# Value projections computed with tokens on the partitions, 512 weight columns per matmul

## The chip, the core and the metric

The kernel runs on one core of one Trainium2 chip. The metric is the device time of one execution in microseconds, the median of several runs. A profiled execution is one such run with the hardware profiler on; its span, from the first to the last recorded instruction, is a little shorter than the time measured for it.

## What is computed

Two layers of a decoder trunk over 256 tokens of 1024 channels. Each layer has a mixer (three branches A, B and C that share one input projection and are merged by gates) and a mixture-of-experts stage. The part that matters here:

```python
D_MODEL = 1024; SEQ = 256; DEPTH = 2          # BATCH = 1
DA_HEADS = 4;   DA_HEAD_DIM = 64;  DA_WIDTH = 512
SB_HEADS = 8;   SB_HEAD_DIM = 64;  SB_WIDTH = 512
CONV_CH = 512;  CONV_WIDTH = 31
IN_SIZES = (512, 512, 512, 2 * 512, 512, 512, 512, 3 * 1024)

def mixer(h, cos, sin, lambda_init, w_in, ...):
    proj = h @ w_in
    qa, ka, va, ub, qc, kc, vc, gates = jnp.split(proj, IN_SPLITS, axis=-1)
    qa = apply_rope(rms_norm(qa.reshape(B, S, 8, 64), qn_g), cos, sin)
    ka = apply_rope(rms_norm(ka.reshape(B, S, 8, 64), kn_g), cos, sin)
    va = va.reshape(B, S, DA_HEADS, 2 * DA_HEAD_DIM)
    ...
    y_a = diff_attention(qa, ka, va, lam, lambda_init, subln_g) @ w_proj_a
    y_b = conformer_conv(ub, w_dw, b_dw, conv_ln_g, conv_ln_b) @ w_proj_b + b_proj_b
    y_c = stick_breaking(qc, kc, vc) @ w_proj_c          # each (B, S, 8, 64)
    g = jax.nn.sigmoid(gates.reshape(B, S, 3, D_MODEL))
    merged = g[:, :, 0] * y_a + g[:, :, 1] * y_b + g[:, :, 2] * y_c
    return merged @ w_out

def conformer_conv(u, ...):
    a, g = jnp.split(u, 2, axis=-1)
    h = a * jax.nn.sigmoid(g)                  # then a causal depthwise convolution, 31 taps
    ...
    return jax.nn.silu(layer_norm(h, ln_g, ln_b))

for l in range(DEPTH):
    ...
    x = x + g_m * mixer(rms_norm(x, norm_mix_g[l]) * (1 + sc_m) + sh_m, ...)
    x = x + g_f * moe_ffn(rms_norm(x, norm_ffn_g[l]) * (1 + sc_f) + sh_f, ...)
```

`va` and `vc`, two of the eight slices of the input projection, are the values of the two attentions. An attention multiplies its weights, a matrix of keys by queries, with the values, and for that the values lie with the tokens on the partitions.

## The kernel before

**Layout.** Activations lie with channels on the partitions and the 256 tokens along the free dimension: `X[j]` is channel block j (128 channels, 8 blocks) of the normalised input. A block is kept either plain in f32, or as two parts in the fp32r format, `hH` (the rounded value) and `hL` (the rest); `plain(...)` and the table `NAT` say how many blocks are plain: none for the input projection of layer 0, three for that of layer 1. A product of split operands takes three fp32r matmuls (`mmj`: H with H, H with L, L with H), a plain one takes one f32 matmul, which runs as two passes and shows as two records. Weights that need it are split just ahead of use by `split`, into buffers named `WH` (an ACT copy) and `WL` (a DVE subtraction), each 128x512 elements; `NSPLIT` = 5 of them are in rotation, and `ahead` splits as far ahead as the buffers allow. `pieces` lists which pieces of a weight are split, in the order of use.

**Projections.** `proj_chunk` computes one chunk: 128 output channels by 256 tokens, with a 128x128 block of the weight as the stationary operand and `X[j]` as the moving one. Four PSUM banks with the name `psA` take these results. A projection such as `qa` has four chunks.

**Value projections.** `tokmajor(n)` computes the four chunks in the same way, channels on the partitions, copies each pair of them to `vT` (ACT), and then appends `flip_v` to the side work: four transposes on PE (L1056) into a bank of `psS`, `psT` or `psG`, and a copy on ACT into the final tile, with tokens on the partitions.

**Order of the work.** One function, `mixer_body`, writes out the order for each layer. `main()` emits the large matmuls and hands over after each chunk with two numbers, an estimate in microseconds of what the piece costs on PE and on DVE (`CH` for input chunks, `GH` for gate chunks). After each such hand-over a loop at the end of `mixer_body` does three things. It advances each generator in the list `sides` by a step (rotary embedding, attention heads, `sums` of squares, `flip_v`, `conv_norm`). It adds to a balance called `credit`: `credit += rate * pc - dc`. As long as the balance is positive, `fill_one` puts one piece of filler work on DVE and takes its cost off: alternately a row of the modulation product (`mod_fill`, `mod_dot`, L530) and a tap of the depthwise convolution (`conv_fill`, L762 and L765; 124 for each layer). Modulation rows that are due are put in even without credit, and then the balance goes negative. So the numbers handed over decide where fillers stand, and nothing measures the time while this is done.

When `conv_fill` is called once more behind the last tap, it appends `conv_norm` (L789 ff.) to the side work. That is the layer norm and the swish of branch B: the mean by four matmuls with `part`, a subtraction (L795), two squares on ACT (L798), sums over channels (`tok_sum`), eleven small DVE operations in `rsqrt` (L455 to L464), a diagonal (L486), a product with `ones` that spreads it over the partitions, four scalings (L813), four sigmoids on ACT and four products (L820). Its result is `T["ob"]`, the input of branch B.

The sequence of the large pieces is in `FRONT` (layer 0: qa, ka, va, ub, kc, qc, vc; layer 1: qa, va, ka, ub, qc, kc, vc) and `PLAN` (layer 0: acACbB, layer 1: abABcC; a small letter is the gate of a branch, a capital the branch's own projection). Then comes the output projection, `out`, and behind it the norm, the routing and the experts. `branch(br)` waits, while nothing else is emitted, as long as the branch's input does not exist (`yield STALL`); it then splits that input into `oH` and `oL` (L1239), multiplies, and merges the result with the gates (L1255, L1259, L1261).

Each engine executes its instructions in the order in which they were written. The weight transfers are issued by SyncE in an order of their own (`Stream`), five buffers deep.

Of the kernel before, what the change touches and what calls it, by code (L numbers as in the profile page):

```python
# [11 lines left out]
F32 = mybir.dt.float32  # L12
# [156 lines left out]
def trunk(ctx, tc, A, out, dbg=None):  # L169
# [426 lines left out]
    def mixer_body(l, pool, before=None):  # L596
# [6 lines left out]
        def take(k):  # L603
            while not free[k]:
                yield POLL
            return free[k].pop(0)
# [15 lines left out]
        def plain(kind, n):  # L622
            return NAT[l]["g" if n in GATES else "i" if kind == "in" else "o" if kind == "out" else n]

        def pieces(o):
            n = plain(*o[0:2])
            return [o + (hf,) for hf in range(2) if n < (4 if o[0] == "proj" else 4 * hf + 4)]
# [40 lines left out]

        def first_split(o):
            n = plain(*o[0:2])  # L670
            return min(4, n if o[0] == "proj" else max(n - 4 * o[3], 0))
# [7 lines left out]
        def split(o):  # L679
            if l == 0 and o[1] in FRONT[0][0:2]:  # L680
                release(o)
            j = first_split(o)
            H = pool.tile([P, 4, P], F32R, name="WH", bufs=NSPLIT[l])
            Lo = pool.tile([P, 4, P], F32R, name="WL", bufs=NSPLIT[l])
            src = weights(o)[:, j:]
# [365 lines left out]
        def flip_v(n, c, vT):  # L1051
            tag = yield from take("ps")
            bt = bank(tag)
            for t in range(NT):
                for k in range(2):
                    pe.transpose(out=bt[:, t * S + k * P:t * S + (k + 1) * P], in_=vT[:, k, t * P:(t + 1) * P],  # L1056
                                 identity=ident)
            yield .9, 0
            se.activation(T["t" + n][:, :, c * S:(c + 1) * S], c2(bt), AF.Copy)
            give("ps", tag)  # L1060
            if c == 1:
                T[n] = T["t" + n]

        def tokmajor(n):
            T["t" + n] = pool.tile([P, 2, 512], F32, name=n)
            for c in range(2):
                b = bank("A")
                for k in range(2):
                    proj_chunk(n, 2 * c + k, b)
                    if k == 0:  # L1070
                        yield CH
                vT = pool.tile([P, 2, S], F32, name="vT", tag="sg", bufs=4)
                se.activation(vT, c2(b), AF.Copy)
                yield CH
                sides.append(flip_v(n, c, vT))
# [17 lines left out]
        CH, GH = ((2.77 + .11 * NAT[l][k], 1.2 - .14 * NAT[l][k]) for k in "ig")  # L1093
        STALL = (.6, 0)
# [835 lines left out]
```

## Time and profile before

| | |
|---|---|
| median of 3 runs | 1621.5 us (1621.37 to 1621.63) |
| profiled execution, its own time | 1622.29 us |
| its span | 1620.7 us |
| PE busy | 1555.2 us (96%), 9710 instructions |
| DVE busy | 751.5 us (46%) |
| ACT busy | 469.1 us (29%) |
| DMA queue q1 | 542.31 MB, 82.5% of 16 engines' span |
| chain of work that ended last | PE 53%, DMA 40%, DVE 4% |

The shares are averages over two layers, each with a mixer and an experts' stage. Seen in 40 slices of the span, PE and DVE are both busy in the first fifth (the mixer of layer 0) and again around the middle (the mixer of layer 1), while the DMA rate falls there to 53 and 97 GB/s; in the rest, the experts, the transfers run at about 420 GB/s and DVE is busy for a fifth of the time. The matmuls of one line (L198, the helper that records every matmul) are told apart by their tiles.

### The profile page before, as it was taken

The numbers are of one execution on the slowest core, as the hardware profiler recorded it, in microseconds if no ns is written. First come the engines' busy times: TensorE is split into PE (matmuls) and PEld (weight loads), VectorE is DVE, ScalarE is ACT, GpSimd is POOL, SyncE is SP. The second block draws the span as 40 slices with busy tenths as digits, with TensorE's granted clock in tenths as the row PEclk, the third lists the DMA queues.
The fourth block names the chain that finished last, engine by engine and source line by source line (L and its number), as shares of the span: only waits on it lengthen the run. The fifth ranks groups of instructions, "written<-read, shape, count | busy, mean of one in ns | idle before, by whom it ended". The sixth has DMA issues, their size and how long they took to land.

```text
span 1620.7 us, 25003 instructions
## 1 busy us (share of the span) xinstructions
PE 1555.2 (96%) x9710; PEld 1050.0 (65%) x9710; DVE 751.5 (46%) x1866; ACT 469.1 (29%) x911; POOL 2.9 (0%) x26
## 2 busy tenths in 40 slices
PE   6999999999999999899989999999999999999997
PEld 5999869974554545454478888798745454554543
DVE  8799989652221222122249998554422222221122
ACT  3546833431111111111144355243211111111111
POOL 0000000000000000000000000000000000000000
PEclk9999979999999999999989999899999999999999
DMA  9985418959999999999958753256599999999997
GB/s 378 366 325 220 156 53 338 386 225 381 408 419 419 420 418 419 421 420 419 414 234 344 276 211 115 97 216 270 201 378 420 419 421 419 418 419 422 420 418 301
DMA packets 76154, 543.95 MB, mean 336 GB/s; under 512 B 8576, under 2 KB 9216, under 8 KB 12544
## 3 DMA queue, kind: packets, MB, share of 16 engines
q1 hardware_dynamic: 76032, 542.31, 82.5%
q8 instruction: 78, 1.28, 0.3%
q14 instruction: 44, 0.36, 0.1%
HBM read 541.23 MB, written 1.05 MB: 335 GB/s over the span
## 4 chain that ended last, share of the span: by engine, by line
PE 53%; DMA 40%; DVE 4%; ACT 1%; issue 1%; SPq 0%; DVEq 0%; ACTq 0%
PE psA L198 30%; DMA wx<-in_w_dram 24%; DMA w<-in_w_dram 15%; PE psT L198 10%; PE psS L198 8%; PE psG L198 4%; DMA w<-in_w_mod_dram 1%; DVE w L530 1%; DVE WL L687 1%; DMA xT<-in_xT_dram 0%; DVE room L765 0%; ACT h L585 0%; DMA w<-in_w_in_dram 0%; ACT WH L686 0%; PE psT L1675 0%
## 5 line engine op out<-in xcount | busy, mean ns | idle before, releaser
L198 PE MATMUL psT<-w,xe 128*64 128x512 f32 (+2 forms) x1216 | 244.5, 594 | 9.6 <-DMA w<-in_w_dram 9.5
L198 PE MATMUL psA<-hH,WH 128*128 128x256 f32 x696 | 210.3, 302 | 0.8 <-ACT WH L686 0.8
L1711 DVE SCALAR_TENSOR_TENSOR Y<-psS,gt,Y 128x512 fp32r<-128x512 f32 x108 | 81.1, 751 | 272.7 <-ACT Y L1710 272.7
L686 ACT ACTIVATE WH<-w 128x512 fp32r<-128x512 f32 (+2 forms) x272 | 147.8, 553 | 203.2 <-PE psA L198 183.7
L1659 DVE TENSOR_SCALAR oT<-psG,slot 128x256 fp32r<-128x256 f32 x54 | 26.1, 484 | 387.9 <-PE psG L198 387.9
L198 PE MATMUL psA<-hH,WL 128*128 128x256 f32 x696 | 197.7, 284 | 1.3 <-DVE WL L687 1.3
L198 PE MATMUL psA<-hL,WH 128*128 128x256 f32 x696 | 197.4, 284 | 0.7 <-DVE hL L575 0.7
L198 PE MATMUL psT<-wx,xe 128*64 128x512 f32 (+2 forms) x832 | 185.7, 594 | 5.6 <-DMA wx<-in_w_dram 5.6
L687 DVE TENSOR_TENSOR WL<-w,WH 128x512 fp32r<-128x512 f32 (+2 forms) x272 | 157.0, 589 | 58.7 <-ACT WH L686 58.0
L198 PEld LDWEIGHTS psT<-w,xe 128*64 128x64 f32 (+2 forms) x1216 | 76.4, 126 | 149.0 <-issue 125.6
L198 PE MATMUL psA<-room,w 128*128 128x256 f32 x592 | 146.1, 391 | 1.1 <-ACT room L578 1.1
L1710 ACT ACTIVATE Y<-psS,gt 128x512 fp32r<-128x512 f32 x108 | 74.4, 689 | 228.1 <-PE psS L198 228.1
L198 PEld LDWEIGHTS psA<-hH,WH 128*128 128x128 f32 x696 | 132.8, 191 | 4.7 <-ACT WH L686 2.4
L198 PEld LDWEIGHTS psA<-hL,WH 128*128 128x128 f32 x696 | 132.8, 191 | 3.0 <-DVE hL L575 0.9
L198 PEld LDWEIGHTS psA<-hH,WL 128*128 128x128 f32 x696 | 132.6, 190 | 2.2 <-DVE WL L687 2.1
L198 PEld LDWEIGHTS psT<-wx,xe 128*64 128x64 f32 (+2 forms) x832 | 64.1, 131 | 103.7 <-issue 101.3
L1649 ACT ACTIVATE sl<-psT 128x256 f32<-128x256 f32 x54 | 20.7, 384 | 368.7 <-PE psT L198 368.7
L198 PEld LDWEIGHTS psA<-room,w 128*128 128x128 f32 x592 | 110.0, 195 | 17.4 <-issue 2.9
L198 PE MATMUL psA<-oT,Y 128*128 128x256 f32 x864 | 116.0, 286 | 0.9 <-ACT Y L1710 0.8
L530 DVE SCALAR_TENSOR_TENSOR w<-w,room 128x1024 f32<-128x1024 f32 x96 | 115.5, 1218 | 1.7 <-DMA w<-in_w_mod_dram 1.6
L198 PEld LDWEIGHTS psA<-oT,Y 128*128 128x128 f32 x864 | 105.7, 189 | 3.7 <-ACT Y L1710 3.4
L765 DVE SCALAR_TENSOR_TENSOR room<-room,tcol,room 128x256 f32<-128x256 f32 x240 | 103.7, 478 | 0.0
(582 smaller groups left out, 2108.4 us busy)
## 6 DMA issues: line engine op xcount, KB each, us to landing
w<-in_w_dram SPq DMA_DIRECT2D x208, 1024.0 KB, 19.9
wx<-in_w_dram SPq DMA_DIRECT2D x152, 1024.0 KB, 19.8
w<-in_w_in_dram SPq DMA_DIRECT2D x56, 1024.0 KB, 8.1
w<-in_w_mod_dram SPq DMA_DIRECT2D x48, 1024.0 KB, 9.0
wx<-in_w_dram SPq DMA_DIRECT2D x6, 2048.0 KB, 22.3
w<-in_w_out_dram SPq DMA_DIRECT2D x8, 1024.0 KB, 7.8
w<-in_w_proj_a_dram SPq DMA_DIRECT2D x4, 1024.0 KB, 7.9
w<-in_w_proj_c_dram SPq DMA_DIRECT2D x4, 1024.0 KB, 6.1
```

What stands on the lines that cost most here:

```text
L198: pe.matmul(out=o, lhsT=lhsT, rhs=rhs, start=start, stop=stop, skip_group_check=True)
L530: ve.scalar_tensor_tensor(t[:, j], t[:, j], 1.0, crow, op0=OP.mult, op1=OP.mult, accum_out=modv[l][:, c:c + 1])
L686: se.activation(H[:, j:], src, AF.Copy)
L687: ve.tensor_tensor(Lo[:, j:], src, H[:, j:].bitcast(F32), op=OP.subtract)
L765: ve.scalar_tensor_tensor(yv[:, ch], hp[:, ch, w:w + S], wc, yv[:, ch], op0=OP.mult, op1=OP.add)
L1649: se.activation(sl, b[:, 0:FF], AF.Silu)
L1659: ve.tensor_scalar(oT, bg[:, 0:S], slot[:, k_:k_ + 1], None, op0=OP.is_equal)
L1710: se.activation(Y[:, hf], b, AF.Copy, scale=gt)
L1711: ve.scalar_tensor_tensor(Y[:, 2 + hf], b, gt, Y[:, hf].bitcast(F32), op0=OP.mult, op1=OP.subtract)
```

## The change

`tokmajor` is written anew. The tokens become the stationary operand: for each channel block j and each half t of the tokens, `X[j][:, 128 t : 128 t + 128]` is loaded, and the whole row block j of the weight, 512 columns, moves through the array. The result stands at once with the tokens on the partitions, in two `psA` banks that are held for the length of the projection, one for each half of the tokens. `flip_v` with its transposes, the tile `vT` and its copies go; two ACT copies at the end write the value tile. The pieces of the weight that are split are now the row blocks j (128x512) and no longer halves of a column chunk, listed in pairs by `pieces`; in layer 1 those are five pieces instead of eight. The hand-overs carry a new pair of numbers, `VH`, after every second block.

```diff
--- before.py
+++ after.py
@@ -623,6 +623,9 @@
             return NAT[l]["g" if n in GATES else "i" if kind == "in" else "o" if kind == "out" else n]
 
         def pieces(o):
+            if o[1] in ("va", "vc"):
+
+                return [("in", o[1], j, 2) for j in range(2 * o[2], 2 * o[2] + 2) if j >= NAT[l]["i"]]
             n = plain(*o[0:2])
             return [o + (hf,) for hf in range(2) if n < (4 if o[0] == "proj" else 4 * hf + 4)]
 
@@ -666,6 +669,9 @@
                 return wget((kind, n)).rearrange("p (j f) -> p j f", j=4)[:, :, c0:c0 + P]
             return wget((kind, hf)).rearrange("p (j f) -> p j f", j=4)[:, :, c * P:(c + 1) * P]
 
+        def rows_of(o):
+            return wget(o[0:2]).rearrange("p (j f) -> p j f", j=KC)[:, o[2]]
+
         def first_split(o):
             n = plain(*o[0:2])
             return min(4, n if o[0] == "proj" else max(n - 4 * o[3], 0))
@@ -679,9 +685,15 @@
         def split(o):
             if l == 0 and o[1] in FRONT[0][0:2]:
                 release(o)
-            j = first_split(o)
             H = pool.tile([P, 4, P], F32R, name="WH", bufs=NSPLIT[l])
             Lo = pool.tile([P, 4, P], F32R, name="WL", bufs=NSPLIT[l])
+            if o[3] == 2:
+                H, Lo = (t.rearrange("p a b -> p (a b)") for t in (H, Lo))
+                src = rows_of(o)
+                se.activation(H, src, AF.Copy)
+                ve.tensor_tensor(Lo, src, H.bitcast(F32), op=OP.subtract)
+                return H, Lo
+            j = first_split(o)
             src = weights(o)[:, j:]
             se.activation(H[:, j:], src, AF.Copy)
             ve.tensor_tensor(Lo[:, j:], src, H[:, j:].bitcast(F32), op=OP.subtract)
@@ -1048,31 +1060,28 @@
                 for _ in range(C_GAP[l]):
                     yield 0, 0
 
-        def flip_v(n, c, vT):
-            tag = yield from take("ps")
-            bt = bank(tag)
+        def tokmajor(n):
+            v = pool.tile([P, 2, 512], F32, name=n)
+            bs = [bank("A") for _ in range(NT)]
+            nat = NAT[l]["i"]
+            for j in range(KC):
+                o = ("in", n, j, 2)
+                w = (rows_of(o),) if j < nat else split_of(o)
+                for t in range(NT):
+                    x = [p[:, t * P:(t + 1) * P] for p in X[j]]
+                    terms = [(x[0], w[0])] if j < nat else [(x[0], w[0]), (x[1], w[0]), (x[0], w[1])]
+                    for k, (a, m) in enumerate(terms):
+                        mm(bs[t], a, m, start=j == 0 and k == 0, stop=j == KC - 1 and k == len(terms) - 1)
+                if j >= nat:
+                    ahead(oidx[o] + 1 + NSPLIT[l])
+                elif j == nat - 1:
+                    st.held.discard(st.pos["in", l, n])
+                if j % 2 and j < KC - 1:
+                    yield VH
             for t in range(NT):
-                for k in range(2):
-                    pe.transpose(out=bt[:, t * S + k * P:t * S + (k + 1) * P], in_=vT[:, k, t * P:(t + 1) * P],
-                                 identity=ident)
-            yield .9, 0
-            se.activation(T["t" + n][:, :, c * S:(c + 1) * S], c2(bt), AF.Copy)
-            give("ps", tag)
-            if c == 1:
-                T[n] = T["t" + n]
-
-        def tokmajor(n):
-            T["t" + n] = pool.tile([P, 2, 512], F32, name=n)
-            for c in range(2):
-                b = bank("A")
-                for k in range(2):
-                    proj_chunk(n, 2 * c + k, b)
-                    if k == 0:
-                        yield CH
-                vT = pool.tile([P, 2, S], F32, name="vT", tag="sg", bufs=4)
-                se.activation(vT, c2(b), AF.Copy)
-                yield CH
-                sides.append(flip_v(n, c, vT))
+                se.activation(v[:, t], bs[t], AF.Copy)
+            T[n] = v
+            yield VH
 
         def sums(i, c, sq):
             yield 0, 0
@@ -1091,6 +1100,7 @@
             yield 0, .2
 
         CH, GH = ((2.77 + .11 * NAT[l][k], 1.2 - .14 * NAT[l][k]) for k in "ig")
+        VH = (2.6 + .11 * NAT[l]["i"], 1.2 - .14 * NAT[l]["i"])
         STALL = (.6, 0)
 
         def quads(ns):
```

**PE, projection `va` of layer 0.** `psA` is the bank of the projection, `psS`, `psT` and `psG` hold the sums of squares of the queries and keys. Before:

```order
L198 MATMUL psA<-hH,WH 128x256
L198 MATMUL psA<-hL,WH 128x256
L198 MATMUL psA<-hH,WL 128x256
L198 MATMUL psS_581<-halves,room_81 128x2 x4
L198 MATMUL psS_586<-halves,room_81 128x2 x4
L198 MATMUL psT<-halves,room_79 128x2 x4
L198 MATMUL psG<-halves,room_79 128x2 x4
L198 MATMUL psA<-hH,WH 128x256
```

and after:

```order
L198 MATMUL psA<-WH,hH 128x512
L198 MATMUL psA<-WH,hL 128x512
L198 MATMUL psA<-WL,hH 128x512
L198 MATMUL psS_557<-halves,room_81 128x2 x4
L198 MATMUL psS_562<-halves,room_81 128x2 x4
L198 MATMUL psT<-halves,room_79 128x2 x4
L198 MATMUL psG<-halves,room_79 128x2 x4
L198 MATMUL psA<-WH,hH 128x512
```

The two operands have changed places and the matmuls are twice as wide; the sums now stand after 24 of the 48 wide matmuls, where 48 of the 96 narrow ones stood ahead of them.

**PE, branches A, C and B of layer 0.** `room_79,w` is branch A and then branch C; `part`, the `ones` with 128x1 and the `ones` with 128x128 are the mean, the sums and the spread of `conv_norm`; `hH,WH` at the end is the first matmul of gate b. Before:

```order
L198 MATMUL psG<-room_78,room_79 64x256
L198 MATMUL psG<-room_78,room_79 64x128
L198 MATMUL psS_2464<-room_80,part 128x256 x4
L198 MATMUL psA<-room_79,w 128x256 x16
L198 MATMUL psT<-ones,room_78 128x1 x8
L198 MATMUL psA<-room_79,w 128x256 x24
L198 MATMUL psS_2563<-room_80,ones 128x128 x2
L198 MATMUL psA<-room_79,w 128x256 x24
L198 MATMUL psA<-hH,WH 128x256
```

After, the end of gate b and the first matmul of branch B (`oH,WH`):

```order
L198 MATMUL psA<-hH,WH 128x256
L198 MATMUL psA<-hL,WH 128x256
L198 MATMUL psA<-hH,WL 128x256
L198 MATMUL psT<-room_80,part 128x256 x4
L198 MATMUL psG<-ones,room_78 128x1 x8
L198 MATMUL psS_2776<-room_80,ones 128x128 x2
L198 MATMUL psA<-oH,WH 128x256
```

The three products of `conv_norm` have moved from the start and middle of branch A to a place behind branches A and C and the 192 matmuls of gate b; the 64 products of A and C stand in one piece in the changed order.

**DVE, the same part of `conv_norm`.** L795, L813, L820, L1239 of before are L807, L825, L832, L1249 after (L1255 is L1265, L687 is L699). Before:

```order
L765 SCALAR_TENSOR_TENSOR room_80<-room_78,tcol_72,room_80 128x256 x4
L986 SCALAR_TENSOR_TENSOR room_79<-room_79,sub_354,psS_2439 128x512
L765 SCALAR_TENSOR_TENSOR room_80<-room_78,tcol_72,room_80 128x256
L986 SCALAR_TENSOR_TENSOR room_79<-room_79,sub_354,psS_2452 128x512
L530 SCALAR_TENSOR_TENSOR w,modv_161<-w,room_81 128x1024 x2
L795 TENSOR_TENSOR room_80<-room_80,psS_2464 128x1024
L530 SCALAR_TENSOR_TENSOR w,modv_161<-w,room_81 128x1024 x2
L1259 TENSOR_TENSOR room_81<-psA,room_81 128x512
```

After, where branch B's input is finished:

```order
L486 TENSOR_TENSOR room_80<-ident,rsy 128x256
L825 SCALAR_TENSOR_TENSOR room_80<-room_80,tcol_72,psS_2776 128x256 x4
L832 SCALAR_TENSOR_TENSOR room_80<-room_80,tcol_72,room_78 128x256 x4
L1249 TENSOR_TENSOR oL<-room_80,oH 128x512
L530 SCALAR_TENSOR_TENSOR w,modv_162<-w,room_81 128x1024
L1249 TENSOR_TENSOR oL<-room_80,oH 128x512
L530 SCALAR_TENSOR_TENSOR w,modv_162<-w,room_81 128x1024 x2
L699 TENSOR_TENSOR WL<-w,WH 128x512 x2
L1265 SCALAR_TENSOR_TENSOR room_80<-psA,tcol_72,room_80 128x256 x2
```

Before, the subtraction L795 came right behind the norm of branch A (L986) and ahead of the first merge (L1259); after, the whole of `conv_norm` stands directly ahead of `oL`, with a modulation row (L530) between the two halves of `oL` and two behind them. Up to the last `rsqrt` of branch A's norm in layer 0, 107 taps are placed before and 102 after, with 40 modulation rows and 88 `WL` subtractions in both.

## Rows read from the trace of the kernel before

**Rows 1.** Busy time by stretch (columns: us, engines, granted clock, DMA share, GB/s)
```profile
130.00:203.00 73.00, 73.00 (x544) 64.78 (x545) 68.74 (x179) 55.96 (x106) 0.00 (x0) 1.00 0.46 174
203.00:230.00 27.00, 24.06 (x110) 15.80 (x109) 23.64 (x66) 11.24 (x25) 0.00 (x0) 0.68 0.00 1
1006.00:1045.00 39.00, 37.84 (x194) 30.26 (x192) 18.02 (x50) 11.82 (x26) 0.00 (x0) 0.87 0.14 54
```
**Rows 2.** The chain (start, us, what) in the experts; busy time by stretch ahead
```profile
421.28 15.49 DMA w<-in_w_dram
...
340.00:345.00 5.00, 5.00 (x28) 3.92 (x27) 3.64 (x16) 0.25 (x1) 0.00 (x0) 1.00 0.00 0
```
**Rows 3.** The chain, runs of matmuls; timeline (start, us), two neighbours of 128 columns
```profile
81.44 11.39 PE psA L198 x96
229.51 6.91 PE psA L198 x32
71.77 0.87 PE psS L198 x2
...
1588.51 0.27 PE L198 MATMUL psG<-oh,htH 128*128 128x128 f32 x1
1588.62 0.28 PE L198 MATMUL psG<-oh,htL 128*128 128x128 f32 x1
```
**Rows 4.** The chain, transposes of a value projection in layer 1
```profile
858.30 0.44 PE psS L1056 x4
858.74 0.44 PE psT L1056 x4
```
**Rows 5.** Timeline of PE in `va`, layer 0 (in brackets: idle before, releaser)
```profile
77.70 0.39 PE L198 MATMUL psA<-hH,WL 128*128 128x256 f32 x1 [1.12 <-DVE WL L687]
```
**Rows 6.** Layer 0 ahead of branch A: timeline of DVE and PE, chain
```profile
203.64 2.05 DVE L765 SCALAR_TENSOR_TENSOR room<-room,tcol,room 128x256 f32<-128x256 f32 x5
217.11 0.58 PE L973 MATMUL psT<-ident,rsy 128*4 128x128 f32 x2 [2.64 <-DVE rsy L464]
226.42 3.09 PE psS L198 x8
```
**Rows 7.** Timeline of PE behind the `halves` sums of layer 0
```profile
62.00 0.41 PE L198 MATMUL psA<-hH,WL 128*128 128x256 f32 x1
62.21 0.41 PE L198 MATMUL psA<-hH,WH 128*128 128x256 f32 x1
```
**Rows 8.** `conv_norm`: layer 0's token sums in the chain, then layer 1's timeline and chain
```profile
236.42 1.68 PE psT L198 x16
1020.78 1.22 DVE L795 TENSOR_TENSOR room<-room,psT 128x1024 f32<-128x1024 f32 x1 [3.46 <-PE psT L198]
1022.10 0.63 ACT L798 ACTIVATE room<-room 128x512 f32<-128x512 f32 x1 [4.17 <-DVE room L795]
1025.27 0.16 DVE L455 TENSOR_SCALAR rsv<-psG 128x2 f32<-128x2 f32 x1 [2.60 <-PE psG L198]
1026.64 0.16 DVE L464 SCALAR_TENSOR_TENSOR rsy<-rst,rsy 128x2 f32<-128x2 f32 x1
1029.95 0.42 DVE L486 TENSOR_TENSOR room<-ident,rsy 128x256 f32<-128x256 f32 x1
1039.67 0.45 PE psS L198 x4
1044.97 0.47 PE L198 MATMUL psA<-oH,WH 128*128 128x256 f32 x1
```
**Rows 9.** Timeline, layer 0: branch B's first matmul, a modulation row, out's second chunk
```profile
282.25 0.28 PE L198 MATMUL psA<-oH,WH 128*128 128x256 f32 x1
290.85 1.22 DVE L530 SCALAR_TENSOR_TENSOR w<-w,room 128x1024 f32<-128x1024 f32 x1
298.96 0.59 PE L198 MATMUL psA<-room,w 128*128 128x256 f32 x2
```
**Rows 10.** Timeline of PE in layer 1, behind the value projection of attention A
```profile
887.48 0.27 PE L857 MATMUL psT<-ident,rsy 128*8 128x128 f32 x1 [1.02 <-DVE rsy L464]
```

## The prediction, made before the changed kernel was run

> **What bounds the kernel now.** I read the stretches of the two mixers first, as busy time of each engine [rows 1]. From 130 to 203 us PE has work in every microsecond at the full clock, and DVE is nearly full too, 68.7 of 73 us: a matmul saved there is time saved only as long as DVE keeps up. Behind it, 203 to 230, PE has lost a tenth of its time to waits and its mean granted clock is 0.68; the same stretch of layer 1, 1006 to 1045, stands at 0.87. Next I looked at what a moved mixer end would do. The expert weights bound the later part of each layer (the chain has the transfer of `w` as its releaser), but they start only once the mixer and the routing are done: between 340 and 345 nothing moves on the DMA engines [rows 2]. So a microsecond gained or lost in either mixer goes to the end one for one, and the sum is made of the two mixers alone.
>
> Then the pace of TensorE [rows 3]. 96 single-pass matmuls of 256 columns took 11.39 us, 119 ns each; two of 128 columns stand 110 ns apart. Halving the columns saves next to nothing, so these are paced by the instruction and not by the columns. 32 f32 products of 256 columns took 6.91 us, 216 ns each, and two f32 ones of 512 columns 435 ns each: an f32 product runs its columns twice, so 512 passes cost 216 ns. That is the nearest row to a single-pass matmul of 512 columns, which this kernel has nowhere.
>
> **What the matmuls save.** In layer 0 a value projection goes from 96 matmuls of 256 columns to 48 of 512. A pair cost 238 ns and its successor 216 by the estimate, so 48 x 22 ns = 1.06 us for each of `va` and `vc`. In layer 1, 30 pairs of split products save 0.66 us, and the three plain rows nothing (f32 at either width is paced by its columns). The step's bounds are 119 ns (the pace per instruction goes on) and 238 ns (proportional). I take 216, the one row with the same number of passes.
>
> The eight transposes of a projection go: two groups of 0.44 us [rows 4], 0.88 us of PE for each projection. Two of the four copies on ACT go as well, and in layer 1 three of the eight splits; ACT and DVE have time for either of them there, so I count these at nothing.
>
> Not all of that arrives. At 77.70 PE waits 1.12 us for a `WL` from DVE [rows 5], so the transposes' share of `va` in layer 0 is lost in a longer wait. That leaves 1.1 + 1.1 + 0.9 = 3.1 us of lead in layer 0. The planner places five convolution taps fewer ahead of branch A's last rsqrt, 5 x 0.41 = 2.0 us of DVE (five taps in 2.05 us [rows 6]), but DVE was 94% busy and PE waits there for DVE's `rsy`, 2.64 us at 217.11 [rows 6]. I take **-2.5** at that point (bounds -1 and -4).
>
> **What moves in layer 0.** The order of the changed kernel shows the larger effect. The sums of `conv_norm` stood around branch A; now they stand behind all of gate b and directly ahead of branch B, which needs their result. On PE this first removes work from the tail. The `part` product cost 3.09 us [rows 6] for eight records which at full clock would be 8 x 0.216 = 1.73: the granted clock was at its lower level (1.2 GHz) after the waits for `rsy`. It leaves with its hand-over, -2.9. But then the first microseconds of branch A stand in that place. That the lower clock paces matmuls is seen behind the `halves` sums, where two neighbouring 256-column matmuls stand 0.21 us apart instead of 0.119 [rows 7]. Three microseconds at that pace hold half the work, +1.6 (bounds 0 and +3). The token sums, 1.68 us, and the spread, 0.45 (as in layer 1 [rows 8]), leave too: -2.1. Gate b so ends 2.5 + 2.9 - 1.6 + 2.1 = **5.9 us earlier**.
>
> There the chain begins for which PE has nothing left to do. Its lengths are in [rows 8]: `part` 1.73; the subtraction 1.22; two squares on ACT of 0.63, 1.26; the half of the sums that must wait for the second square, 0.84; eleven small rsqrt steps on DVE (the eighth starts 1.37 us after the first, 0.196 each), 2.15; the diagonal 0.42; the spread 0.45. Together 8.1, and with six hand-overs of some 0.07 us 8.5. From the spread to branch B's first matmul layer 1 shows 4.85 us, from 1039.67 + 0.45 to 1044.97: four scalings, four sigmoids, four products, the split of `o`. So B starts about 13.35 us after gate b ends; before it started at once. Behind that start, B and out's first chunk took 282.25 to 298.96, 16.7 us [rows 9], paced by DVE's merges and splits and by `w_mod` rows at 1.22 us. In the new order one such row stands between the two halves of `oL` and two behind them. I add 0.45 for it. Bounds: -3 if splits made during the wait shorten B, +1.9 if the row lies fully in front of it. Sum **+13.8**.
>
> Layer 0: -5.9 + 13.8 = **+7.9** (range +4 to +11). What hid this chain before was branch A and C's 64 products and gate b's 192 matmuls; all that cover is now ahead of it.
>
> **Layer 1.** `va` saves 0.66 + 0.88 = 1.5, of which the wait of 1.02 us for `rsy` at 887.48 [rows 10] will take a part: -1.0. `vc` -1.5. The spread now stands behind branch A's last product, ahead of B, and B waits for scalings and products that A's last eight matmuls and branch C's heads used to hide: +3.5 (the 4.85 us above less what gates and heads still cover; bounds 0 and +4.85). The sums around A fall into places where PE already waited for ACT, -2. Sum **-1.0** (range -4 to +2).
>
> Both together: +6.9. The profiled execution took 1622.29 us, of it a span of 1620.7 and 1.59 around it; the median of the runs is 1621.5, 0.79 less. On the median: 1621.5 + 6.9 = **1628.4 us**.
>
> The Trainium skill, "TensorE: Matmul & The Clock Gate", section "Back-to-back issue gap", gives columns / 2.4 + 2.5 ns for matmuls in a row at full clock: 109 ns at 256 columns and 216 at 512. The second agrees with the 216 that 512 passes take here; the first does not agree with the measured 119. By the page's two figures a pair would save 2.6 ns, not 22, and the sum would be 156 x 19.4 ns = 3.0 us higher, an estimate of 1631.4.
>
> **Rivals.** (a) *The wait repays itself.* While PE stands idle for 13 us, DVE and ACT split the weights of B and out ahead, so B runs at PE's pace (-3), and A's start finds the full clock (-1.6): +6.9 - 4.6 = +2.3, 1623.8 us. For it: B's 16.7 us hold 96 matmuls of 0.119 = 11.4 of PE work alone. Against it: only five split buffers exist, so at most five pieces are ahead, and the merges stay on DVE. Chance 0.20.
>
> (b) *512 columns cost 238 ns.* Then nothing is saved: 156 matmuls x 22 ns = 3.4 more, 1631.8. Against it are the 216 ns per 512 passes. Chance 0.11.
>
> (c) *The other side: the pace of an instruction goes on at 512 columns*, 119 ns. Then 156 x 97 ns = 15.1 us more are saved, 1613.3, faster than before. It decides from a step below 216 - 6.9/156 = 172 ns on. For it: 128 and 256 columns cost nearly the same. Against it: an f32 product of 512 columns takes 435 ns, just what two passes of 512 columns at 216 take; nothing in the trace moves columns faster. Chance 0.07. The Trainium skill, same page and section, states some 131 ns for a sustained matmul of 512 columns; by that figure the sum would be 13.3 us lower, an estimate of 1615.1. No row here shows such a pace, and the f32 rows speak against it.
>
> That the change doesn't do what it says is no case here: the order holds the 512-column matmuls and no transposes of `vT`.
>
> **How the numbers follow.** Forecast 0.62, (a) 0.20, (b) 0.11, (c) 0.07. The unknown costs of the forecast (step and clock, +4 to +11 in layer 0, -4 to +2 in layer 1, rarely at the same end) reach from some 1623 to 1634; (a) and (b) lie in or near that; only (c) is left out, with the edges. Range 1619 to 1635. A measurement of this kernel can tell about 0.2% from no change, which is 1618.3 to 1624.7: (a) lies within it, the forecast and (b) above, (c) below. Faster 0.07, same 0.20, slower 0.73.
>
> **What would show it.** In the changed profile: 512-column matmuls 216 ns apart; PE idle some 11 to 13 us ahead of the first `oH` product in layer 0, released by DVE and ACT, with `part`, sums and spread in the gap; gate b's end some 6 us earlier (near 276); the mixer's end in layer 0 about 8 later, in layer 1 about 1 earlier relative to its start. A gap under 8 us, or a step below 172 ns, would make the prediction wrong.

## The result

The changed kernel took 1638.5 us (median of 7 runs) against 1623.65 for the kernel before (7 runs): ratio 1.0085, 95% interval 1.0066 to 1.0105, slower by some 13.8 us. A second round gave 1.0078 (1.0059 to 1.0097), 12.7 us. The forecast was slower by 6.9 us, a ratio of 1.0043: the sign was right, the size half of it, and the time lies above the stated range. The runs of one kernel spread over some 10 us here, so what follows rests on ratios with their intervals and on stages within profiles. The kernel before, run once more as if it were a new one, read 0.9986 (0.9970 to 1.0002); nothing smaller than 0.2% is read as a difference below.

The profiled execution of the changed kernel took 1638.83 us, its span 1637.2. The page's first line for it:

```profile
PE 1557.3 (95%) x9498; PEld 1038.5 (63%) x9498; DVE 751.9 (46%) x1860; ACT 469.7 (29%) x901; POOL 2.9 (0%) x26
```

212 matmul records fewer than before, yet PE is no less busy, in a span 16.5 us longer. Where the time lies is seen in layer 0, from the end of gate b to the end of branch B. Busy time by stretch, changed kernel (columns as in [rows 1]): the tail ahead of branch A, the wait ahead of branch B, branch B itself; then layer 1's way from `part` to B, and B.

```profile
207.10:230.00 22.90, 18.88 (x92) 11.61 (x91) 18.50 (x56) 10.45 (x23) 0.00 (x0) 0.71 0.01 1
282.40:295.40 13.00, 5.03 (x30) 4.09 (x28) 7.25 (x22) 4.66 (x9) 0.00 (x0) 0.73 0.36 149
295.40:310.30 14.90, 14.62 (x95) 14.04 (x96) 13.07 (x26) 5.89 (x10) 0.00 (x0) 0.78 0.92 369
1033.80:1060.00 26.20, 23.53 (x111) 19.46 (x110) 11.60 (x31) 6.13 (x14) 0.00 (x0) 0.89 0.17 63
1060.00:1073.50 13.50, 13.35 (x99) 13.06 (x99) 10.54 (x20) 4.65 (x9) 0.00 (x0) 0.88 0.45 171
```

and the tail and branch B of layer 0 in the kernel before:

```profile
203.40:229.40 26.00, 23.06 (x104) 14.88 (x103) 22.79 (x64) 11.24 (x25) 0.00 (x0) 0.67 0.00 1
282.30:293.70 11.40, 11.40 (x97) 11.40 (x97) 9.71 (x19) 6.41 (x11) 0.00 (x0) 1.00 1.02 422
```

The second row is the exposed chain: 13 us in which PE works for 5. The third is the surprise: branch B's 96 matmuls took 14.9 us instead of 11.4, with PE busy nearly all the time and a granted clock of 0.78 instead of 1.00 (a mean over the stretch; the levels are 1.2 and 2.4 GHz, 0.50 and 1.00). The timeline of PE shows where the level changes: the matmuls of B start 0.21 us apart up to 301.9, and 0.12 us apart from there.

```profile
301.28 0.41 PE L198 MATMUL psA<-oL,WH 128*128 128x256 f32 x1
301.49 0.41 PE L198 MATMUL psA<-oH,WL 128*128 128x256 f32 x1
...
302.24 0.27 PE L198 MATMUL psA<-oH,WH 128*128 128x256 f32 x1
302.35 0.28 PE L198 MATMUL psA<-oL,WH 128*128 128x256 f32 x1
```

The timeline of the chain, changed kernel (start, us; in brackets the idle time before and its releaser), which answers to [rows 8]:

```profile
282.37 1.89 PE L198 MATMUL psT<-room,part 128*128 128x256 f32 x8
284.30 1.22 DVE L807 TENSOR_TENSOR room<-room,psT 128x1024 f32<-128x1024 f32 x1 [0.49 <-PE psT L198]
286.30 1.95 PE L198 MATMUL psG<-ones,room 128*128 128x1 f32 x16 [2.04 <-ACT room L810]
288.28 0.16 DVE L455 TENSOR_SCALAR rsv<-psG 128x2 f32<-128x2 f32 x1 [2.76 <-PE psG L198]
290.44 0.43 DVE L486 TENSOR_TENSOR room<-ident,rsy 128x256 f32<-128x256 f32 x1
290.92 1.23 PE L198 MATMUL psS<-room,ones 128*128 128x128 f32 x4 [2.68 <-DVE room L486]
292.26 1.66 DVE L825 SCALAR_TENSOR_TENSOR room<-room,tcol,psS 128x256 f32<-128x256 f32 x4 [1.40 <-PE psS L198]
293.83 1.67 DVE L832 SCALAR_TENSOR_TENSOR room<-room,tcol,room 128x256 f32<-128x256 f32 x4
295.43 0.58 PE L198 MATMUL psA<-oH,WH 128*128 128x256 f32 x1 [3.28 <-ACT oH L1248]
```

PE waits three times, 2.04, 2.68 and 3.28 us, in the order the forecast gave. The wide matmuls of `va` at the start, and the wait that answers to [rows 5] (it lies in `ub`, the projection behind `va`, in both kernels, and not in `va`), changed kernel, timeline of PE:

```profile
51.98 0.39 PE L198 MATMUL psA<-WH,hH 128*128 128x512 f32 x1
52.21 0.40 PE L198 MATMUL psA<-WH,hL 128*128 128x512 f32 x1
...
57.33 0.40 PE L198 MATMUL psA<-WL,hH 128*128 128x512 f32 x1
...
78.82 0.39 PE L198 MATMUL psA<-hH,WL 128*128 128x256 f32 x1 [2.00 <-DVE WL L699]
```

From the first to the last of these 24 wide matmuls are 23 steps in 5.35 us: 232 ns each, where a pair of narrow ones took 238. And the wait for `WL` has grown from 1.12 to 2.00, by just the 0.88 us of the transposes.

### The profile page after: what moved, and what is told of

Same layout as the page of the kernel before. It is cut to its first block, busy times and chain, and to the rows that moved or that the text cites. A ratio compares the mean times of both kernels' runs of the same rounds, so it can differ in the third digit from the quotient of the medians.

```text
span 1637.2 us, 24557 instructions
## 1 busy us (share of the span) xinstructions
PE 1557.3 (95%) x9498; PEld 1038.5 (63%) x9498; DVE 751.9 (46%) x1860; ACT 469.7 (29%) x901; POOL 2.9 (0%) x26
## 4 chain that ended last, share of the span: by engine, by line
PE 31%; DMA 29%; DVE 1%; ACT 1%; issue 1%; SPq 0%; DVEq 0%; ACTq 0%
DMA wx<-in_w_dram 18%; PE psA L198 16%; DMA w<-in_w_dram 11%; PE psT L198 7%; PE psS L198 5%; PE psG L198 3%; PE psT L1685 0%; DVE w L530 0%; DVE WL L699 0%; ACT h L585 0%; PE psS L947 0%; DVE nt L584 0%; DVE xT L1740 0%; SPq L242 0%; SPq L251 0%
## 5 line engine op out<-in xcount | busy, mean ns | idle before, releaser
L698 ACT ACTIVATE WH<-w 128x512 fp32r<-128x512 f32 (+2 forms) x240 | 131.2, 552 | 221.7 <-PE psA L198 203.4
L198 PE MATMUL psA<-hH,WH 128*128 128x256 f32 x592 | 179.8, 304 | 0.0
L198 PE MATMUL psA<-hH,WL 128*128 128x256 f32 x592 | 168.5, 285 | 2.0 <-DVE WL L699 2.0
L198 PE MATMUL psA<-hL,WH 128*128 128x256 f32 x592 | 168.3, 284 | 0.1
L699 DVE TENSOR_TENSOR WL<-w,WH 128x512 fp32r<-128x512 f32 (+2 forms) x240 | 138.3, 589 | 54.7 <-ACT WH L698 54.2
L198 PE MATMUL psA<-room,w 128*128 128x256 f32 x544 | 135.7, 395 | 1.1 <-ACT room L578 1.1
L530 DVE SCALAR_TENSOR_TENSOR w<-w,room 128x1024 f32<-128x1024 f32 x96 | 115.4, 1218 | 1.2 <-DMA w<-in_w_mod_dram 1.1
L198 PEld LDWEIGHTS psA<-hH,WH 128*128 128x128 f32 x592 | 113.4, 192 | 3.5 <-ACT WH L698 0.9
L198 PEld LDWEIGHTS psA<-hL,WH 128*128 128x128 f32 x592 | 113.4, 192 | 2.6 <-issue 1.0
L198 PEld LDWEIGHTS psA<-hH,WL 128*128 128x128 f32 x592 | 113.2, 191 | 2.6 <-DVE WL L699 2.6
L198 PEld LDWEIGHTS psA<-room,w 128*128 128x128 f32 x544 | 102.8, 198 | 17.5 <-issue 2.8
```

The source lines that it names most:

```text
L198: pe.matmul(out=o, lhsT=lhsT, rhs=rhs, start=start, stop=stop, skip_group_check=True)
L530: ve.scalar_tensor_tensor(t[:, j], t[:, j], 1.0, crow, op0=OP.mult, op1=OP.mult, accum_out=modv[l][:, c:c + 1])
L698: se.activation(H[:, j:], src, AF.Copy)
L699: ve.tensor_tensor(Lo[:, j:], src, H[:, j:].bitcast(F32), op=OP.subtract)
```

## The experiments

Theory 1 at the start: the loss is the exposed `conv_norm` chain, and the lower clock behind it. Theory 2: the wide form itself brings PE to the lower clock in the projections. All ratios are to runs of the kernel before on the same chip in the same round.

**e1, the norm early again.** In the changed kernel:

```diff
-        VH = (2.6 + .11 * NAT[l]["i"], 1.2 - .14 * NAT[l]["i"])
+        VH = (3.22 + .11 * NAT[l]["i"], 1.2 - .14 * NAT[l]["i"])
```

> The new value projections stay; only their hand-over number for PE goes from 2.6 to 3.22, so that the planner places conv_norm's mean, sums and spread around branch A again, as in the kernel before. Theory 1 (the loss is the exposed conv_norm chain and the lower clock behind it): the 12.9 us wait ahead of branch B goes, B takes 11.6 us again and not 15.2, the tail takes its 5 us of part, sums and spread back; total 1619 to 1623 us, ratio to the kernel before 0.998 to 1.001. Theory 2 (the 512-column form itself brings PE to the lower clock in the projections, +3.7 us at the end of gate c): the wait goes as well but the +3.7 stays, ratio 1.002 to 1.004.

Measured: 1.0037 (1.0019 to 1.0055). The wait ahead of B was gone and B took 11.3 us, as theory 1 said; but the ratio lies within the bounds of theory 2. The profile shows another cause in layer 0, though its run was the fastest of the twelve (1619.7 us, median 1629.3). Timeline, ahead of branch A:

```profile
210.01 6.81 DVE L777 SCALAR_TENSOR_TENSOR room<-room,tcol,room 128x256 f32<-128x256 f32 x17
216.74 0.16 DVE L455 TENSOR_SCALAR rsv<-psS 128x8 f32<-128x8 f32 x1
221.77 0.59 PE L985 MATMUL psS<-ident,rsy 128*4 128x128 f32 x2 [4.43 <-DVE rsy L464]
```

The larger number gave the planner credit for 17 taps in a row, and the rsqrt of branch A's norm stands behind them: PE waits 4.43 us where it had waited 2.64 [rows 6]. So this run had changed two things.

**e2, the norm late, narrow form.** In the kernel before, within `tokmajor`:

```diff
-                        yield CH
+                        yield VB if l == 0 else CH          # and so at the second yield
...
+        VB = (2.0, 1.2)
```

> The kernel before with its narrow value projections, but with their hand-over number lowered in layer 0 so that conv_norm stands behind gate b, as in the changed kernel. Theory 1: the exposed chain costs by itself 13 us of wait and some 3 us at the lower clock in B, less some 3.5 us of tail: +12 to +13 us, ratio 1.0075 to 1.008. Theory 2: the order alone is worth the 13.35 less 5.9 of the forecast, +7 to +8, ratio 1.0045.

Measured: 1.0078 (1.0062 to 1.0094), +12.7 us; 13.1 us of wait and 14.6 in B. Without a single wide matmul the order costs as much as the whole change.

**e3, throwaway matmuls in the wait.** In the changed kernel, in `branch`:

```diff
+                busy = l == 0 and br == "b"
                 while "o" + br not in T:
+                    for _ in range(8 if busy else 0):
+                        mm(bank("A")[:, 0:S], identb, tri)
                     yield STALL
+                for _ in range(20 if busy else 0):
+                    mm(bank("A")[:, 0:S], identb, tri)
```

> The changed kernel with 68 throwaway bf16 matmuls of 256 columns (into psA, never read) in the wait ahead of branch B of layer 0: 16 behind part, 24 behind the sums, 28 behind the spread. Theory 1 (B takes 15.2 us instead of 11.6 because the clock is at its lower level when it starts): granted clock 1.0 in B, B 11.6 to 12.5 us, total 3 us under the changed kernel. Rival (B is paced by DVE's modulation rows and splits): B stays at 15 us, no difference.

Measured: 1.0061 (1.0045 to 1.0077), which the intervals do not tell from the changed kernel. Its stretches, wait and B, and B's first rows in the timeline of PE:

```profile
280.60:294.10 13.50, 12.78 (x105) 10.84 (x104) 8.34 (x25) 4.63 (x9) 0.00 (x0) 1.00 0.37 149
294.10:308.70 14.60, 13.48 (x96) 13.08 (x97) 13.09 (x26) 5.88 (x10) 0.00 (x0) 0.88 0.93 368
```

```profile
294.10 0.38 PE L198 MATMUL psA<-oH,WH 128*128 128x256 f32 x1 [0.40 <-ACT oH L1253]
294.83 0.39 PE L198 MATMUL psA<-oL,WH 128*128 128x256 f32 x1 [0.35 <-DVE oL L1254]
296.58 0.44 PE L198 MATMUL psA<-oL,WH 128*128 128x256 f32 x1 [0.76 <-DVE oL L1254]
```

The clock held at 1.00 through the wait and fell in B less than before, to 0.88 instead of 0.78; but B took 14.6 us, not 12. Two waits for `oL` have come out, 0.35 and 0.76, the second behind the modulation row that stands between the halves of `oL`. In the timeline of the changed kernel, where the matmuls ahead of them run at the lower clock, they do not show. 14.9 us there are 11.4 at the full clock plus the lower clock: 22% of 14.9, 3.3. In this run it is 12% of 14.6, 1.8, and 1.1 of waits; some 0.3 us are left over. So B's growth is the clock in the changed kernel, and taking the clock away alone buys back less than it cost.

**e4, the changed kernel again; e5, the kernel before again.**

> The changed kernel a second time, for a second profile. Its runs so far lie at 1630 to 1634 and at 1638 to 1642 us. If the difference is the place where the clock falls, the waits (ahead of B 12.9 us, ahead of branch A's norm) are the same and the granted clock in 60:90, 200:207 and 295:311 differs; if it is something else, the clock is the same and another stretch has moved. Ratio 1.0085 again.

> The kernel before a second time, for a second profile of it. If the lower clock behind the sums of va (3.4 us in the first profile, 6.8 us in the profiles of both the changed kernel and of the narrow kernel with the late norm) is scatter between runs, some profiles of before show 6.8 us too and gate c then ends 2 us later than at 203.15; if it comes with the wide matmuls it is 3.4 again. Ratio 1.000.

Measured: 1.0078 (1.0059 to 1.0097), and 0.9986 (0.9970 to 1.0002). e4's waits are those of the first profile, 12.9 us ahead of B, and B 14.9; but gate c ended 2.2 us earlier, since two stretches at the lower clock in the projections were missing. The kernel before showed the same front in both profiles; the narrow e2, whose front stands on PE in the same order, was 2.2 us late there. So this part is scatter between runs, and theory 2 cannot be read from one profile.

**e6 and e7, two other hand-overs.** In the changed kernel 2.6 becomes `(2.75, 2.6)[l]` for e6 and `(2.9, 2.6)[l]` for e7, in layer 0 alone.

> The wide value projections with the layer-0 hand-over number for PE at 2.75 (2.6 in the change), layer 1 as in the change. By the written order part now stands between branches A and C, the sums within C, the spread behind C, and gate b's 192 matmuls cover the rest; no part in the tail and 104 taps ahead of the rsqrt of branch A's norm (102 in the change, 107 before). Theory (exposed chain and B behind it cost 16.5 us, the form saves 2.5 at the norm): 12.5 us less than the changed kernel, 3 us less than the kernel before, ratio 0.997 to 0.999. Rival (the form itself costs, as the 1.0037 of the run with the early norm suggests): 1.003 or more.

> As the run before with 2.9: the order of part, sums and spread around branches A and C is that of the kernel before word for word, and 107 taps stand ahead of the rsqrt of branch A's norm as there (112 in the run with the early norm, 3.22, whose tail was 30.7 us instead of 26.2). Theory: the wide form by itself, -2.5 in layer 0 and -1 to +1 in layer 1, ratio 0.997 to 1.000; the 1.0037 of the early-norm run was the five further taps ahead of the rsqrt. Rival (the form itself costs): 1.003.

Measured: 1.0016 (0.9999 to 1.0033) and 1.0031 (1.0012 to 1.0051). Both are well under the changed kernel, so the place of the norm is most of the loss; but both miss the theory's number by some 0.3%, 5 us, as e1 did. They keep the change's order in layer 1, which the next run takes alone.

**e8, the change in layer 1 alone** (`tokmajor` as before for l == 0, and `pieces` likewise).

> The wide value projections in layer 1 alone, layer 0 as in the kernel before. The forecast gave layer 1 -1.0 us (range -4 to +2): ratio 0.9994, at most 0.9975 to 1.0012. If layer 1 holds a part of what came on top of the forecast, it is 1.002 or more.

Measured: 1.0014 (0.9997 to 1.0031): 2.3 us slower and not the gain of 1 us that the forecast had there, but not clear of no difference.

**e9, the wide form with the plan of the kernel before.** This run was to tell whether the missing 5 us of e7 belong to the form or to the order. In the changed kernel:

```diff
+        def ghost():
+            tag = yield from take("ps")
+            yield .9, 0
+            give("ps", tag)
...
                 if j % 2 and j < KC - 1:
-                    yield VH
+                    yield CH
+                    if j == 3:
+                        sides.append(ghost())
...
-            yield VH
+            yield CH
+            sides.append(ghost())
```

> The wide value projections, but with the hand-overs of the kernel before: CH four times for each projection, and a side step without instructions where each flip_v stood. On PE the order of layer 0 is then word for word that of the kernel before, except that the matmuls of va and vc are wide and the transposes are gone. Theory A (the form saves, and every loss comes from the order that the planner wrote with the new numbers): -2.5 us or a little more in layer 0, ratio 0.997 to 0.999. Theory B (the PE time saved is given back by longer waits on DVE and by the lower clock that follows them): end of gate c and the tail as late as in the kernel before or later, ratio 1.000 to 1.003.

Measured: 0.9986 (0.9970 to 1.0001). Theory A: the form does no harm, and with the old order the loss is gone. Against e7, which has the same wide matmuls and the same order of `part`, sums and spread, it is 0.45% faster, some 7 us. What differs is the other side work that the new numbers had moved. Timeline of PE ahead of branch A, e7:

```profile
220.51 0.58 PE L985 MATMUL psS<-ident,rsy 128*4 128x128 f32 x2 [2.96 <-DVE rsy L464]
222.62 0.87 PE L947 MATMUL psS<-ident,room 128*128 128x128 f32 x3 [1.53 <-DVE room L1030]
224.07 0.87 PE L947 MATMUL psT<-ident,room 128*128 128x128 f32 x3 [0.57 <-DVE room L1030]
```

and e9:

```profile
218.72 0.58 PE L985 MATMUL psT<-ident,rsy 128*4 128x128 f32 x2 [3.04 <-DVE rsy L464]
219.24 1.56 PE L198 MATMUL psS<-room,room 128*64 128x256 f32 x8
220.84 0.87 PE L947 MATMUL psG<-ident,room 128*128 128x128 f32 x3
```

In e7 the last heads of attention C have their transposes right behind the norm, and PE waits 1.53 and 0.57 us for the products they turn; in e9 the value products of earlier heads stand between and the waits are gone. The changed kernel shows the same two waits. Whether these are all of the 7 us is open: 1.9 us of it lie in layer 1, and some in lower-clock stretches that come and go.

**e10, e9 with the transposes kept.** `ghost` issues four transposes of `ones` into its bank.

> The same with the eight transposes of each projection kept as throwaway work (of a constant, into a bank that nobody reads), at the places where flip_v had them: only the width of the matmuls differs from the kernel before. Theory A: the transposes are worth 1.8 us in each layer less the wait in va, so about +1 us to the run without them, ratio 0.998 to 1.000. Theory B: no difference to the run without them, or better than it, since PE is busy where it waits otherwise; ratio 1.000 to 1.002.

Measured: 0.9987 (0.9970 to 1.0004), as e9. With intervals of some 0.16% to either side, 2.6 us, the run times cannot tell the +1 us of theory A from theory B. The profiles show both at work. In layer 0 the wait of [rows 5] is 1.12 us again, where e9 has 2.00: that share is waited away. In layer 1 e10 took 293.0 us from the first `hH` to the end of `out`, e13 and e14 (below) 292.1 and 292.2, with the same order on PE but for the transposes and the same time at the lower clock, 6.8 us: there about half of the transposes' 1.76 us arrives.

**e11 and e12, e9 with the norm moved.** In e9's `tokmajor`, both yields:

```diff
-                    yield CH
+                    yield CH[0] - (.65 if l == 0 else 0), CH[1]     # e11; .45 in e12
```

> The run with the plan of the kernel before (wide matmuls, everything else in the old order), with the layer-0 hand-over of the value projections lowered by 0.65. On PE layer 0 then differs from that run only in the place of part, sums and spread: behind gate b, ahead of branch B, as in the change. By the forecast's own terms this costs 13.8 - 2.9 + 1.6 - 2.1 = +10.4 us: ratio 1.005 to the kernel before. With the wait of 12.9 us and B at the lower clock (+3.3 instead of +0.45), as the profiles of the changed kernel show, +12.5: ratio 1.0063. If the side work's other moves make up most of the change's loss, it is +6 or less, ratio 1.002.

> The same with the hand-over lowered by 0.45: part stands behind the first 16 products of branch A, so it leaves the tail that runs at the lower clock (3.1 us for it there, 1.7 at the full clock), and its chain is still covered by A, C and gate b. Against the run with the plan of the kernel before: -1 to -1.5 us, ratio to the kernel before 0.9975 to 0.999; if the lower clock only moves into A's products instead, no difference to that run, 0.9985 to 0.9995.

Measured: e11 1.0071 (1.0051 to 1.0090), e12 0.9975 (0.9962 to 0.9988). Between e9 and e11 PE's order in layer 0 differs in nothing but the place of three products, and 0.85% lies between them, 13.8 us; the terms of the forecast had given 10.4, with the measured clock of B 12.5. On DVE the norm's operations moved with these products, and the taps too: ahead of branch A's norm PE waits 0.74 us for `rsy` in e11's profile, 3.04 in e9's, so the 13.8 us are the price of the norm's move with all that goes with it on DVE, not of the three products alone. e11's wait and B, by stretch:

```profile
276.00:289.70 13.70, 5.74 (x29) 4.80 (x28) 7.82 (x25) 4.66 (x9) 0.00 (x0) 0.68 0.37 151
289.70:303.80 14.10, 13.82 (x96) 13.23 (x97) 13.06 (x26) 5.90 (x10) 0.00 (x0) 0.83 0.92 363
```

In e12 `part` stands behind sixteen products of branch A. Timeline of PE:

```profile
224.15 8.32 PE L198 MATMUL psA<-room,w 128*128 128x256 f32 x32
232.31 1.89 PE L198 MATMUL psS<-room,part 128*128 128x256 f32 x8
234.03 6.21 PE L198 MATMUL psA<-room,w 128*128 128x256 f32 x28
```

`part` takes 1.89 us here and 3.09 in [rows 6], and its chain is covered by what follows.

**e13, the old plan in layer 1 alone; e14, e12 again.** e13 is the change in layer 0 and e9 in layer 1 (`yield CH if l else VH`, `ghost` only for l == 1).

> Layer 0 word for word as in the change, layer 1 with the wide matmuls but the hand-overs and side steps of the kernel before. The profiles put layer 1 from its first projection to the end of out at 297 us in the change, 297 in the kernel before and 293.5 with the old plan. If the order of layer 1 (the spread behind branch A, B's wait of 2.7 us and the lower clock behind it) takes back what the form saves there, this run lies 3 to 4 us under the change: ratio 1.0055 to 1.0065 to the kernel before. If layer 1 plays no part, 1.008 again.

> The fastest version so far (wide matmuls, old plan, part behind the first 16 products of branch A) a second time: 0.9975 again if it is faster than the kernel before, 0.9986 to 1.000 if that reading was scatter, since the kernel before itself read 0.9986 against its own runs.

Measured: e13 1.0062 (1.0042 to 1.0083), as expected if layer 1's order takes back what the form saves; its interval touches that of the change. By stretch, `part` to B and B in layer 1 of e13:

```profile
1023.40:1049.00 25.60, 25.43 (x121) 20.52 (x120) 11.58 (x31) 6.88 (x16) 0.00 (x0) 0.90 0.00 1
1049.00:1062.00 13.00, 13.00 (x109) 12.48 (x107) 10.79 (x21) 4.66 (x9) 0.00 (x0) 1.00 0.81 301
```

The changed kernel had a wait of 2.67 us ahead of this B, in this profile nothing waits there:

```profile
1059.90 0.58 PE L198 MATMUL psA<-oH,WH 128*128 128x256 f32 x1 [2.67 <-ACT oH L1248]
```

e14: 0.9974 (0.9957 to 0.9991), as e12. Two rounds agree on a version that is faster than both kernels, by some 4 us than the kernel before and by 17 to 18 than the change; that the kernel before read 0.9986 against itself leaves a part of the 4 us open.

The stages side by side, in us, each from the first or last row of its tile in the timeline of PE:

| | before | change | e4 | e9 | e11 | e12 |
|---|---|---|---|---|---|---|
| layer 0, first `hH` to branch A | 189.8 | 190.2 | 187.6 | 192.3 | 185.1 | 184.6 |
| branch A to end of gate b | 53.1 | 52.6 | 52.7 | 53.1 | 51.4 | 55.8 |
| wait ahead of branch B | 0 | 12.9 | 12.9 | 0 | 13.6 | 0 |
| branch B | 11.4 | 14.9 | 14.9 | 11.4 | 14.0 | 11.3 |
| out | 28.6 | 28.4 | 28.4 | 28.6 | 28.3 | 29.0 |
| layer 1, first `hH` to end of out | 296.8 | 297.7 | 296.9 | 293.5 | 293.4 | 293.4 |

Each column is a single profile, and the place where the clock falls moves its stages. The profiled run of e9 was the slowest of its twelve (1627.25 us, median 1620.3), with 27 us at the lower clock ahead of branch A where the kernel before has 20.5; its 192.3 in the first line does not show a cost of the form. And layer 1 of the kernel before, with the same order on PE and DVE, took 296.8 us in both profiles of that kernel but 293.6 in e2's. The difference lies ahead of branch B, in the stretch that [rows 1] shows with 39.00 us and a clock of 0.87; in e2:

```profile
1022.40:1058.20 35.80, 34.64 (x193) 28.23 (x192) 17.96 (x50) 11.81 (x26) 0.00 (x0) 0.95 0.16 59
```

## Why the prediction was right in its sign and too small

**What bounds the kernel.** Right: the mixer of layer 1 ended 15.6 us later in the changed kernel's profile than in that of the kernel before, and the span is 16.5 longer.

**The step of a wide matmul.** Mis-sized: 232 ns in layer 0 and 227 to 230 in layer 1, against the 216 that the forecast took; the upper bound of 238 was nearly met. With 156 matmuls that is 2.5 us of the expected gain. The error lay in reading records as products. The 32 records of 6.91 us in [rows 3] are the 16 products of `w` that the written order has between `part` and the sums, two records to each f32 product (that is also how 212 fewer records come about). So 216 ns is one record of 256 columns, a whole f32 product of 256 columns took 432 ns, and the 435 ns taken for a product of 512 columns is one of its two records. None of those rows shows 512 columns in 216 ns; the two narrow fp32r matmuls that the wide one replaces, 238, were the better row. The Trainium skill, "TensorE: Matmul & The Clock Gate", section "Back-to-back issue gap", gives 216 ns at 512 columns too, but the row that seemed to agree was the misread one; this case's 232 decides against it here, and no run shows the 131 ns of the same section.

**The transposes.** The part that was said to be lost was lost to a hundredth (1.12 to 2.00 us of wait, and 1.12 again in e10). Whether the rest arrives the run times of e9 and e10 do not tell; their profiles of layer 1 speak for about half of it there.

**The lead of 2.5 us at branch A's norm.** Not seen in the changed kernel's first profile. The step takes 1.5 of it. The rest depends on the lower clock in the projections: from the first `hH` to the end of gate c they took 163.9 us in the kernel before (mean granted clock 0.99), 167.4 in the change (0.96), 164.8 in e4 (0.98) and 163.2 in e13, which has the change's layer 0 (0.99). The new hand-over numbers also moved not only `conv_norm` but the heads of attention C, which put waits of 1.53 and 0.57 us behind the norm, against which stands a shorter wait for `rsy`, 1.22 instead of 2.64. The order showed the heads; I read it at `conv_norm` alone.

**Tail and branch A.** The tail's -2.9 and branch A's +1.6 - 2.1 hold as sums: the tail takes 22.9 us instead of 26.0, and the stage from A to the end of gate b fell by 0.5 in the change, as summed. That gate b nevertheless ended at 282.5 and not at 276 is the lead above and lower-clock stretches in the projections; e4 ended it at 280.5, e13 at 278.8, and e11, with the old side order, at 276.1.

**The chain.** Right as a sum: 13.35 forecast, 12.9 measured. `part`, the subtraction, the squares and the rsqrt steps came within 0.2 us; the sums and the spread took longer (1.5 and 1.23 us instead of 0.84 and 0.45), the way from the spread to B was shorter (3.28 instead of 4.85).

**Branch B behind the chain.** This step failed most: +0.45 forecast, +3.5 measured. I had counted the lower clock for branch A, which follows a stretch of waits, and not for branch B, which follows one with more waiting (PE idle for 8 of 13 us, against 3 of 26 in the tail before). The rows for it stood in the profile of before: 0.68 in the stretch with waits [rows 1], and the slow pair behind the `halves` sums [rows 7].

**Layer 1.** -1.0 forecast, 0 to +0.9 in the two profiles of the change against the two of the kernel before. Other profiles with the same order on PE widen both sides: 295.4 to 298.9 us with the change's layer 1 (e3, e6, e7, e8), 293.6 with the narrow one (e2). So one profile gives this term to some 3 us, and its sign stays open. The form does save there with the old plan: e9 took 293.5 us and the kernel before 296.8, both with 10.2 us at the lower clock. But in the change the spread's new place gives a wait of 2.67 us and a B at 0.88.

With the two mis-sized terms, 6.9 + 2.5 for the step + 3.05 for B - 0.45 for the chain = 12.0 us, near the 12.7 to 13.8 measured; the remainder lies within the interval. That it comes so near is in part luck: with the step put right the forecast has gate b end near 278 us, and the two profiles of the change have 282.5 and 280.5.

**The rivals.** (a), the wait that repays itself, did not come: B ran slower and not faster behind it. (b), the step at 238, was nearly the truth as to the step. (c), the pace of 119 ns, is ruled out by 232; the f32 row that was held against it was misread, as said above.

## What to carry to other kernels

Where an order is planned from cost numbers, a change of such a number moves everything that is filled in after it: compare the two orders at every place where an engine waited, not just at the largest move. Price such a change twice, once with the old order kept (here 0.9986) and once as it is (1.0085), since the form and its side effects are separate. And when a wait is put into the stream of TensorE, count what follows it at the lower clock as well: 3.5 us here on top of a wait of 12.9.

## What the hardware showed that was not expected

A single-pass fp32r matmul of 512 columns took 232 ns, hardly less than two of 256 columns, 238; an f32 product of 256 columns, two records of 216 ns [rows 3], took 432. The clock was at its lower level until 6.5 us into branch B, whose 96 matmuls keep PE busy for 14.6 of 14.9 us, after a stretch in which PE had been busy for 5 of 13 us; with throwaway matmuls in that stretch the granted clock in it was 1.00, and still fell to 0.88 in B.
